# Carrying each half of the partitions on its own DMA queue, in 512-step chunks, in a matmul with a decayed running sum

## The chip, the cores and the metric

One core of a Trainium2 chip. The metric is the device time of one execution in microseconds (us), as the median of several runs. A shorter time is better.

## The reference

```python
B, S, D = (16, 2048, 1024)           # x: B x S x D, w: D x D, decay: D, all float32
xw = x @ w
out[:, 0, :] = xw[:, 0, :]
for t in range(1, S):
    out[:, t, :] = decay * out[:, t - 1, :] + xw[:, t, :]
```

x is 134 MB and so is the output; both have to pass between memory and SBUF once.

## The kernel before

The four quadrants of 32 partitions each hold a quarter of the channels. x comes in as float32 tiles `xf` of 512 time steps, ScalarE casts them to bfloat16 (`xb`), VectorE transposes them in 32x32 blocks (`xt`, the "input transpose"), TensorE multiplies with the weights into PSUM (`ps`), VectorE runs the decayed sum along time (the "scan", into `so`) and transposes back (`ot`, the "output transpose"), and `ot` is stored. A unit is 1024 steps of all 1024 channels: eight values of `n`, 16 matmuls each. All loads of x are issued on SyncE's queue, all stores on ScalarE's.

```python
def load(u, l):                                  # 512 steps: 2 MB
    xf = xfp.tile([128, 2, NI, CQ], FP32, name="xf")              # 3 buffers
    for r in range(2):
        for q in range(NQ):
            nc.sync.dma_start(out=xf[q * P:(q + 1) * P, r], in_=...)
    xb = xbp.tile([128, NI, CQ, 2], BF16, name="xb")              # 2 buffers
    for r in range(2):
        nc.scalar.copy(out=xb[:, :, :, r], in_=xf[:, r])
# ... turn(u, l): VectorE transposes xb into xt
for u, (b, h) in enumerate(units):
    for n in range(K):                           # K = 8
        ps = psp.tile([128, TU], FP32, name="ps")
        for k in range(K):
            for l in range(NL):
                nc.tensor.matmul(out=ps[:, l * TL:(l + 1) * TL], ...)
        # ... scan ps into so; keep its last column for the next unit
        if prev is not None:
            flush(prev)                          # output transpose of the scan before
            if n == 0:
                store(u - 1, prev[1])            # 4 dma_start on nc.scalar
        prev = (so, ot, n)
        if n == 1 and u + 1 < len(units):
            turn(u + 1, 0)
            load(u + 1, 1)
        if n == 5 and u + 1 < len(units):
            turn(u + 1, 1)
            if u + 2 < len(units):
                load(u + 2, 0)
```

The program's order is not the order on an engine: when the program is built, a scheduler places the instructions of each engine, VectorE's above all. In the profiles `ACTq` and `SPq` mark the issuing of transfers by ScalarE and SyncE, and `out_dram<-ot` is a store, `xf<-in_x_dram` a load of x.

## Time and profile before

| | before |
|---|---|
| median (lowest to highest) | 1121.59 us (1121.13 to 1122.7, 4 runs) |
| VectorE busy | 1013.7 us, 90% |
| TensorE busy | 932.3 us, 83% |
| ScalarE busy | 324.1 us, 29% |
| moved by DMA | 273.33 MB, mean 243 GB/s |
| 300 to 1060 us: VectorE busy, DMA | 752.47 of 760 us, 261 GB/s |

An engine's share of the whole span hides the stages: from 300 us on VectorE works without a pause, and its losses lie at the two ends. The lines behind this are in the prediction.

### The profile page before, as it was taken

The page shows a single profiled execution, that of the slowest core. Times are in us where ns is not written, and L with a number is a line of the kernel's source. Part 1 is how long each engine was busy: PE and PEld are TensorE (multiplying, and loading weights), DVE is VectorE, ACT ScalarE, POOL GpSimd, SP SyncE. Part 2 cuts the span into 40 slices and gives each one's busy share as a digit, 9 for nine tenths or more (in the row PEclk, how much of TensorE's full clock was granted, in tenths as well). Part 3 has the DMA queues.
Part 4 walks back from the last instruction along what each step waited for, and adds up shares of the span by engine and source line. Part 5 has one row for each costly group of instructions (what it writes and reads, how often), then busy time and mean ns, then how long its engine had stood idle before and what let it go on. Part 6 is the DMA issues. An engine that isn't in the chain of part 4 may idle for free.

```text
span 1123.0 us, 10242 instructions
## 1 busy us (share of the span) xinstructions
PE 932.3 (83%) x4096; PEld 408.4 (36%) x4096; DVE 1013.7 (90%) x584; ACT 324.1 (29%) x257; POOL 0.2 (0%) x4
## 2 busy tenths in 40 slices
PE   0287698796998998989898998989898998989880
PEld 0133243242443443434343443434343443434330
DVE  1295699798999999999999999999999999999991
ACT  2124122242422405151422405151422405151200
POOL 0000000000000000000000000000000000000000
PEclk9997799797999998999999899989999898999995
DMA  9949898999999999999999999999999999999777
GB/s 194 203 81 228 163 268 198 260 275 252 283 272 276 252 276 260 249 273 266 279 264 252 259 279 269 252 274 266 271 264 259 256 277 247 274 278 236 150 145 155
DMA packets 275056, 273.33 MB, mean 243 GB/s; under 512 B 11840, under 2 KB 273984, under 8 KB 275008
## 3 DMA queue, kind: packets, MB, share of 16 engines
q1 hardware_dynamic: 140800, 138.45, 55.5%
q10 hardware_dynamic: 134208, 134.23, 45.5%
q8 instruction: 32, 0.52, 0.2%
q14 instruction: 16, 0.13, 0.0%
HBM read 138.42 MB, written 134.22 MB: 243 GB/s over the span
## 4 chain that ended last, share of the span: by engine, by line
DVE 41%; DMA 27%; issue 9%; SPq 8%; PE 7%; ACTq 3%; ACT 2%; DVEq 0%
DVE so L141 24%; DMA xf<-in_x_dram 15%; DVE ot L115 11%; DMA out_dram<-ot 11%; SPq L91 8%; PE ps L133 7%; DVE xt L106 6%; ACTq L169 3%; ACT xb L97 2%; DMA xf<-in_w_dram 1%; DMA dec<-in_decay_dram 1%; SPq L76 0%; ACT keep L151 0%; ACTq L64 0%; DVE wsb L77 0%
## 5 line engine op out<-in xcount | busy, mean ns | idle before, releaser
L133 PE MATMUL ps<-xt,wsb 128*128 128x512 bf16 x4096 | 932.3, 389 | 157.7 <-DVE xt L106 95.0
L133 PEld LDWEIGHTS <-wsb 128*128 128x128 bf16 x4096 | 408.4, 100 | 681.0 <-issue 204.2
L97 ACT CAST xb<-xf 128x2048 bf16<-128x2048 f32 x128 | 310.8, 2474 | 306.2 <-DVE ot L115 100.3
L115 DVE STREAM_TRANSPOSE ot<-so 128x1024 f32<-128x1024 f32 x256 | 309.3, 1224 | 3.7
L141 DVE TENSOR_TENSOR_SCAN so<-dec,ps 128x1024 f32<-128x1024 f32 x128 | 285.3, 2252 | 20.6 <-PE ps L133 20.6
L141 DVE TENSOR_TENSOR_SCAN so<-dec,keep,ps 128x1024 f32<-128x1024 f32 x128 | 295.1, 2306 | 6.4 <-PE ps L133 6.4
L106 DVE STREAM_TRANSPOSE xt<-xb 128x2048 f32<-128x2048 f32 x64 | 146.2, 2285 | 44.6 <-ACT xb L97 42.7
L151 ACT COPY keep<-so 128x1 f32<-128x1 f32 x128 | 21.1, 186 | 429.7 <-DVE so L141 329.5
L77 DVE CAST wsb<-xf 128x1024 bf16<-128x1024 f32 x8 | 5.4, 687 | 9.8 <-DMA xf<-in_w_dram 9.8
L97 ACT ACT_TABLE_LOAD x1 | 1.3, 1283 | 8.8 <-DMA xf<-in_x_dram 8.8
L190 POOL MEMSET const-uint8-127<- 128x1 uint8 x1 | 0.1, 102 | 0.0
L190 POOL MEMSET const-bfloat16-1.0<- 128x1 bf16 x1 | 0.1, 101 | 0.0
L190 POOL MEMSET const-float32-0.0<- 128x1 f32 x1 | 0.1, 98 | 0.2 <-issue 0.2
L190 POOL MEMSET const-float32-1.0<- 128x1 f32 x1 | 0.1, 98 | 0.0
## 6 DMA issues: line engine op xcount, KB each, us to landing
xf<-in_x_dram SPq DMA_DIRECT2D x512, 256.0 KB, 8.3
out_dram<-ot ACTq DMA_DIRECT2D x128, 1024.0 KB, 13.3
xf<-in_w_dram SPq DMA_DIRECT2D x32, 128.0 KB, 4.0
dec<-in_decay_dram ACTq DMA_DIRECT2D x4, 1.0 KB, 5.6
```

Of the source, the lines that this page charges most:

```text
L77: nc.vector.tensor_copy(out=wsb[:, k].rearrange("p n q i -> p q n i"), in_=wv.rearrange("p (q n i) -> p q n i", q=NQ, n=K))
L91: nc.sync.dma_start(out=xf[q * P:(q + 1) * P, r], in_=_ap(x, [[2 * D, P], [64 * D, NI], [1, CQ]], (b * S + t0 + r) * D + q * CQ))
L97: nc.scalar.copy(out=xb[:, :, :, r], in_=xf[:, r])
L106: nc.vector.transpose(out=dst.rearrange("p k (i t) -> p i k t", t=P), in_=src.rearrange("p (i k t) -> p i k t", k=K, t=P))
L115: nc.vector.transpose(out=ot[:, :, n * P:(n + 1) * P], in_=so.rearrange("p (i t) -> p i t", t=P))
L133: nc.tensor.matmul(out=ps[:, l * TL:(l + 1) * TL], lhsT=wsb[:, k, n].rearrange("p q i -> p (q i)"), rhs=xt[:, k, l, :], start=(k == 0), st ...
L141: nc.vector.tensor_tensor_scan(out=so, data0=dec[:, n:n + 1].to_broadcast([128, TU]), data1=ps, initial=0.0 if h == 0 else last[n], op0=AL ...
L151: nc.scalar.copy(out=keep, in_=so[:, TU - 1:TU])
L169: nc.scalar.dma_start(out=_ap(out, [[D, P], [P * D, TU // P], [1, CQ]], (b * S + h * TU) * D + q * CQ), in_=ot[q * P:(q + 1) * P])
L190: nc = _bacc.Bacc("TRN2", target_bir_lowering=False, num_devices=1)
```

## The change

The intent: quadrants 0 and 1 (partitions 0 to 63) are always carried on SyncE's queue and 2 and 3 on ScalarE's, for loads and stores alike, so that the two queues never meet on the same half. The work goes in 512-step chunks; most groups are pairs of chunks (1024 steps, a unit as before), and the first two and last two chunks are groups of their own, so that the first scan starts sooner and the last store is smaller. The first chunk's matmuls run with k outermost, so that they can begin when the first slice of weights has come. Weights are cast on GpSimd, and so are the copies of the carried column.

```diff
+    def queue(q):
+        return nc.sync if q < 2 else nc.scalar
...
-    def load(u, l):
+    def load(c):
...
-            for q in range(NQ):
-                nc.sync.dma_start(
+            for q in (0, 2, 1, 3):
+                queue(q).dma_start(
...
+    groups = [[0], [1]] + [[c, c + 1] for c in range(2, nch - 2, 2)] + [[nch - 2], [nch - 1]]
...
+    def store(g, ot, n0, n1):
...
+        for q in (0, 2, 1, 3):
+            queue(q).dma_start(out=..., in_=ot[quad(q), :, n0 * P:n1 * P])
...
+    for gi, g in enumerate(groups):
...
+        at = {1: after[:1], 5: after[1:]}
...
+            scan(g, n, ps, ot)          # scan, then flush(): output transpose or store pending
+            for c in at.get(n, []):
+                turn(c)
+                if next_load < nch:
+                    load(next_load)     # four dma_start per queue, then two casts on ScalarE
+                    next_load += 1
...
+            pending.append(lambda g=g, ot=ot: store(g, ot, 0, K))
```

## The prediction

> **What bounds the kernel now.** I read the page first, then the busy times by stretch, then VectorE's timeline where the stretches differ, and the chain of waits last.
>
> From the page: busy time and share of each engine, then the costliest groups (busy us, mean ns, idle before, releaser).
>
> ```profile
> PE 932.3 (83%) x4096; PEld 408.4 (36%) x4096; DVE 1013.7 (90%) x584; ACT 324.1 (29%) x257; POOL 0.2 (0%) x4
> ...
> L115 DVE STREAM_TRANSPOSE ot<-so 128x1024 f32<-128x1024 f32 x256 | 309.3, 1224 | 3.7
> L141 DVE TENSOR_TENSOR_SCAN so<-dec,ps 128x1024 f32<-128x1024 f32 x128 | 285.3, 2252 | 20.6 <-PE ps L133 20.6
> ```
>
> VectorE (DVE) is the bound: 1013.7 of 1123.0 us. The by-stretch table says where the other 109 us lie (length, then busy PE, PEld, DVE, ACT, POOL, then granted clock, DMA share, GB/s):
>
> ```profile
> 0.00:46.00 46.00, 1.89 (x4) 0.58 (x5) 7.65 (x9) 10.88 (x5) 0.20 (x4) 1.00 1.00 198
> ...
> 173.00:236.00 63.00, 50.50 (x219) 21.65 (x217) 56.78 (x33) 21.16 (x14) 0.00 (x0) 0.86 0.97 251
> ...
> 428.00:491.00 63.00, 58.05 (x256) 25.50 (x255) 62.35 (x37) 19.48 (x16) 0.00 (x0) 0.96 1.08 266
> ...
> 1095.00:1123.00 28.00, 0.00 (x0) 0.00 (x0) 3.73 (x3) 0.00 (x0) 0.00 (x0) 0.50 0.75 155
> ```
>
> From about 300 to 1064 us VectorE is at 99% and a unit of 1024 steps takes 31.6 us (63.25 us a pair: the stores of two units begin at 376.55, 439.80, 503.24). 38 us are lost before 46 and 24 after 1095; the rest between 46 and 300, where this timeline shows the mechanism that I think decides the case (start, length, engine; idle and releaser in brackets):
>
> ```profile
> 199.99 2.31 DVE L141 TENSOR_TENSOR_SCAN so<-dec,keep,ps 128x1024 f32<-128x1024 f32 x1
> 202.33 1.25 DVE L115 STREAM_TRANSPOSE ot<-so 128x1024 f32<-128x1024 f32 x1
> 202.35 0.59 PE L133 MATMUL ps<-xt,wsb 128*128 128x512 bf16 x1 [2.92 <-DVE so L141]
> 203.50 2.27 DVE L106 STREAM_TRANSPOSE xt<-xb 128x2048 f32<-128x2048 f32 x1
> ...
> 205.82 10.46 PE L133 MATMUL ps<-xt,wsb 128*128 128x512 bf16 x37 [2.88 <-DVE xt L106]
> ...
> 211.57 2.29 DVE L141 TENSOR_TENSOR_SCAN so<-dec,ps 128x1024 f32<-128x1024 f32 x1 [5.80 <-PE ps L133]
> ```
>
> Here the second input transpose (xt) of a unit stands last on VectorE, just ahead of that unit's first scan. TensorE gets past its first matmul only when it is done, and VectorE waits 5.80 us for the 15 others. The same wait is 5.89 at 54.46, 6.40 at 98.31, 5.91 at 139.78. From 300 on it is gone: both xt transposes stand three or more scans before the unit's end (552.27: xt, then four scans in a row without a wait).
>
> **What the Trainium skill says.**
> 1. "TensorE: Matmul & The Clock Gate", Part 1 (the HAM clock gate): after an idle window of about 3.4 us the array runs at half rate until about 3.4 us of sustained work have passed. The trace agrees: the granted clock is 0.59 from 205.8 to 211.6 (17 matmuls) and 1.00 in the 5.4 us after (27). Hence 5.8 us for 15 matmuls, not 15 x 0.22 = 3.3.
> 2. "SBUF — State Buffer", Door 1: partitions 0 to 63 reach eight of the 16 DMA ports, 64 to 127 the other eight. That is the change's reason. The trace fits it: one queue alone moves about 206 GB/s (29 to 44 us), and with both at work stretches of 4 us show either 203 to 215 or 305 to 372, as if queues met on one half or not. The same page ("Can I just issue two DMAs to hit both halves?") says two loads at once gained only 6%; no run here shows that yet.
> 3. "GPSIMD Engine Reference", 3.1: elementwise work takes about twice VectorE's time. VectorE's weight cast is 0.69 us, so I estimate 1.4 us on GpSimd; the trace before has none there.
>
> **The change, part by part.** I also had the changed kernel built and read its instructions in order; the scheduler decides more than the diff.
>
> *VectorE's order* is the main term. Before, the late units run "xt, scan, scan, scan ..." in varied patterns with the transposes early. After, every one of the 30 pair groups has one fixed pattern: scan and output transpose three times, xt for the next group's first chunk, five more of both, xt for its second chunk, next group. The second xt is always immediately ahead of the next group's first scan. TensorE can do one matmul for each of n = 0 to 3 from the first chunk and then must wait, exactly as at 202 to 211 us. So each unit pays the 5.8 us, and TensorE, nearly idle before it, starts cold each time.
> A unit after: eight scans with output transposes, strictly alternating, 3.45 us apart without and 3.51 with a carried state (211.57 to 215.06 and on; 101.86 to 105.37), so 27.6 and 28.1, mean 27.8; two xt at 2.2 = 4.4; wait 5.8. Sum 38.0 us. Cross-check: the unit from 172.26 to 211.57 took 39.3 with one output transpose more (1.13), so 38.2. Against 31.6.
>
> *The start.* Lost: the 1024-step first unit that needs 4 MB of x and 4 MB of weights before it can run well (first scan at 54.46). After: 2 MB of x on two queues; ACT issues the upper weights only behind its casts of x (it runs in order), about 10 to 12 us; two slices fly at once at some 4 us (their landing time now), so eight need 16 us; last cast and k-step 3: first scan at about 31. Eight half-size scans and transposes, half of 3.45 plus 0.15 fixed (estimate): 15 us, to 46. xt of chunk 1 2.2, wait for eight cold matmuls at 0.43: 3.4; second group 15 + 2.2; then xt 2.2 and wait 5.8: first scan of the first pair at 77, where before it is at 98.31. Gain 21.
>
> *The end.* Half-size groups: xt and wait 5.6 once more. The last store is 1 MB on two queues, about 5 us, instead of 24 us for 4 MB on one. Gain 19.
>
> *Off the path.* keep copies go from ACT to GpSimd (128 x 0.19 us; the ACT waits of 329.5 us on the scans were harmless idle time). Casts of weights leave VectorE (5.4 us).
>
> *Sum.* 77, plus 29 units between the 30 first scans at 38.0 = 1102, gives 1179; last pair 27.8 + 2.2, to 1209; chunk 62 15, to 1224; 5.6, to 1230; chunk 63 15, to 1245; store 5: **1250 us**. As a difference: -21 at the start, -19 at the end, 6.4 x 29 = +186, less the 23 us that units lose today (971 us from the scan at 98.31 to that at 1069.64, where 30 x 31.6 is 948), and +7 for the split last unit: +130, the same to 3 us.
>
> **The rivals.**
> (a) *Transfers decide.* In the chain of waits DMA has 27%, and SyncE's queue waits 326.5 us for stores. If balanced ports and the shorter ends were all, VectorE's 1014 plus about 45 of start and 20 of end would make some 1080. Against: VectorE is at 99% in mid-run, where faster DMA gives it nothing, and the built order shows the late xt.
> (b) *ACT becomes the bound.* Its order after is: two stores, four loads, two casts, four loads, two casts. It waits in a cast for a load that it issued itself, so upper loads are never ahead by more than one chunk. Per unit: stores and loads on its ring 3.1 MB at about 206 GB/s 15 us, receipt 2, cast 2.5, then 1 MB 5, receipt 2, cast 2.5: about 30 us, under 38. If it took 42, the total would be some 1370. Against: casts would be ready some 15 us before the late xt.
> (c) *TensorE stays warm.* Then the wait is 3.3 to 3.6 instead of 5.8, 2.3 less x 30: about 1180. Against: it was cold in all four cases cited.
>
> **Range and chances.** The wait of 5.4 to 6.4 moves the sum by -12 to +18; the start by 8; alternation costs by 10; (b) in part adds, (c) in part takes away. 1200 to 1300 should hold it 8 times in 10. Faster by over 2% would need the late xt not to matter, though its order is fixed in the built program: 0.05. Within 2%: 0.04. Slower: 0.91.
>
> **What would show each step.** In the changed profile: VectorE's scan idle before, released by PE, some 170 us over about 30 waits near 5.8 us (now 27.0 in 5); granted clock near 0.6 in each of these gaps; VectorE near 82% busy in mid-run, a unit near 38 us; DMA about 225 GB/s there; first scan near 31 and first 1024-step scan near 77 us; under 10 us from the last transpose to the end. I am wrong if xt waits on ACT's cast instead (rival b), if waits are nearer 3.4 us (c), or if units stay near 32.

## The result, and the profile after

The changed kernel took 1405.03 us (1403.81 to 1405.84, 4 runs) against 1121.59 us: ratio 1.2524, 95% interval 1.2503 to 1.2546. Ratios are computed as the mean time of one kernel's fast runs over that of the other's of the same rounds, so they are not quite the ratio of the medians quoted. The direction was as predicted, but it is 155 us more than the 1250 us, and outside the range.

From the page after: busy time and share, then three groups (busy us, mean ns, idle before, releaser):

```profile
PE 985.0 (70%) x4015; PEld 417.2 (30%) x4096; DVE 1032.8 (74%) x608; ACT 315.8 (23%) x129; POOL 34.9 (2%) x156
...
L99 ACT CAST xb<-xf 128x2048 bf16<-128x2048 f32 x128 | 314.5, 2471 | 1034.9 <-DMA xf<-in_x_dram 905.4
...
L135 DVE TENSOR_TENSOR_SCAN so<-dec,ps 128x1024 f32<-128x1024 f32 (+1 forms) x128 | 279.7, 2186 | 101.2 <-PE ps L123 101.2
...
L105 DVE STREAM_TRANSPOSE xt<-xb 128x2048 f32<-128x2048 f32 x64 | 147.3, 2302 | 156.3 <-ACT xb L99 156.0
```

VectorE has the same work as before, to 20 us, but is busy for 74% of the span. The scans wait for TensorE, as predicted (101.2 us here and 96.1 in the group of carried scans, together 197.3 in 33 waits). What was not predicted is the last line: the input transposes wait 156.0 us for ScalarE's casts, and the casts wait 905.4 us for their loads (94.3 before).

VectorE's timeline of one unit, from the second input transpose of one group to the first scan of the next but one (start, length; in brackets idle and releaser):

```profile
621.21 2.31 DVE L105 STREAM_TRANSPOSE xt<-xb 128x2048 f32<-128x2048 f32 x1
628.86 2.29 DVE L135 TENSOR_TENSOR_SCAN so<-dec,ps 128x1024 f32<-128x1024 f32 x1 [5.33 <-PE ps L123]
...
645.43 2.31 DVE L105 STREAM_TRANSPOSE xt<-xb 128x2048 f32<-128x2048 f32 x1 [6.11 <-ACT xb L99]
...
673.11 2.35 DVE L135 TENSOR_TENSOR_SCAN so<-dec,keep,ps 128x1024 f32<-128x1024 f32 x1 [5.60 <-PE ps L123]
```

At 628.86 is the predicted wait for a cold TensorE. At 645.43 is the other: the *first* input transpose of the group, the one in mid-unit, stands still for 6.11 us until its cast is done. This unit, from 628.86 to 673.11, takes 44.25 us. On average over the run, from the first 1024-step scan at 79.63 to the last group's at 1328.74 us, it is 1249.1 / 29 = 43.1 us, where 38.0 were predicted and 31.6 were needed before.

The chain of waits of the changed kernel says what the cast waited for. It is read from the top down; each line is what released the next (start, length, what):

```profile
619.99 1.25 DVE ot L150
...
621.26 7.04 DMA out_dram<-ot
...
628.66 2.17 ACTq L93
...
630.87 11.98 DMA xf<-in_x_dram
...
642.92 2.49 ACT xb L99
...
645.43 0.04 DVE xt L105
...
663.76 1.26 DVE ot L150
...
665.03 7.03 DMA out_dram<-ot
```

This is a closed loop of 665.03 - 621.26 = 43.8 us: the group's store on SyncE's queue takes 7.0; ScalarE's queue, which was held until then, issues the next loads (2.5 with a small piece left out here); the load takes 12.0, the cast 2.5; then come the input transpose, five scans and their output transposes (VectorE, 18.3 from 645.43 to 663.76, and 1.3 for the last), and the last of these completes the group and allows the next store. A loop that closes on itself sets the pace whatever else the engines could do.

Why a load on ScalarE's queue waits for a store on SyncE's is in the packed trace, which names for each transfer the semaphore that its issue waits for and the one that its completion signals (`prof` doesn't print them). In the built program eight completion semaphores, numbers 99 to 106, serve the transfers of both queues and are used again and again. SyncE's store of 621.26 signals number 99 and lands at 628.30. The second of ScalarE's four loads is the next to use 99; it waits for it and is issued at 628.32, and the third and fourth stand behind it:

```profile
618.73 13.91 ACTq L93 DMA_DIRECT2D xf<-in_x_dram  x4
```

No buffer links this store and these loads. In the whole run 28 loads of ScalarE are issued within 60 ns of the landing of such a store of SyncE; in the kernels below that have the stores behind the loads it is at most 4.

In the two stretches from 300 to 1060 us, before and then after (length, busy PE, PEld, DVE, ACT, POOL with counts, then granted clock, DMA share, GB/s):

```profile
300.00:1060.00 760.00, 696.97 (x3092) 307.05 (x3091) 752.47 (x433) 236.34 (x191) 0.00 (x0) 0.96 1.06 261
```

```profile
300.00:1060.00 760.00, 529.78 (x2153) 223.37 (x2196) 564.81 (x317) 172.36 (x70) 12.65 (x69) 0.83 0.87 193
```

VectorE falls from 99% to 74%, and the transfers from 261 to 193 GB/s, although the change was meant to make them faster. The queues mostly took turns: by the packet records of the trace only SyncE's queue moves data from 622 to 634 us, and only ScalarE's from 644 to 648; in the 760 slices of 1 us each of the two moves over 20 GB/s in 223, one alone in 502. No engine is full: that is the mark of a loop of waits, not of a bound by one engine.

### The profile page after: what moved, and what is told of

It is laid out like the page before. It is cut to its first block, busy times and chain, and to the rows that moved or that the text cites. A ratio compares the mean times of both kernels' runs of the same rounds, so it can differ in the third digit from the quotient of the medians.

```text
span 1402.0 us, 10369 instructions
## 1 busy us (share of the span) xinstructions
PE 985.0 (70%) x4015; PEld 417.2 (30%) x4096; DVE 1032.8 (74%) x608; ACT 315.8 (23%) x129; POOL 34.9 (2%) x156
## 4 chain that ended last, share of the span: by engine, by line
DMA 40%; DVE 39%; issue 8%; ACT 5%; ACTq 4%; PE 2%; SPq 0%; DVEq 0%
DVE so L135 26%; DMA xf<-in_x_dram 25%; DMA out_dram<-ot 14%; DVE ot L150 10%; ACT xb L99 5%; ACTq L93 4%; DVE xt L105 3%; PE ps L123 2%; DMA wf<-in_w_dram 1%; DMA dec<-in_decay_dram 0%; SPq L93 0%; DVEq L233 0%; ACTq L99 0%; SPq L160 0%; DVEq L150 0%
## 5 line engine op out<-in xcount | busy, mean ns | idle before, releaser
L123 PE MATMUL ps<-xt,wsb 128*128 128x512 bf16 x4015 | 985.0, 403 | 405.6 <-DVE so L135 257.9
L123 PEld LDWEIGHTS <-wsb 128*128 128x128 bf16 x4096 | 417.2, 102 | 972.9 <-issue 530.1
L99 ACT CAST xb<-xf 128x2048 bf16<-128x2048 f32 x128 | 314.5, 2471 | 1034.9 <-DMA xf<-in_x_dram 905.4
L135 DVE TENSOR_TENSOR_SCAN so<-dec,keep,ps 128x1024 f32<-128x1024 f32 (+1 forms) x144 | 306.7, 2133 | 97.1 <-PE ps L123 96.1
L135 DVE TENSOR_TENSOR_SCAN so<-dec,ps 128x1024 f32<-128x1024 f32 (+1 forms) x128 | 279.7, 2186 | 101.2 <-PE ps L123 101.2
L150 DVE STREAM_TRANSPOSE ot<-so 128x1024 f32<-128x1024 f32 (+1 forms) x272 | 319.9, 1179 | 8.3
L105 DVE STREAM_TRANSPOSE xt<-xb 128x2048 f32<-128x2048 f32 x64 | 147.3, 2302 | 156.3 <-ACT xb L99 156.0
L145 POOL COPY keep<-so 128x1 f32<-128x1 f32 x144 | 26.4, 183 | 1314.0 <-DVE so L135 1314.0
L76 POOL CAST wsb<-wf 128x1024 bf16<-128x1024 f32 x8 | 8.3, 1037 | 22.7 <-DMA wf<-in_w_dram 22.5
```

Source lines behind the costliest of these rows:

```text
L76: nc.gpsimd.tensor_copy(out=wsb[:, k].rearrange("p n q i -> p q n i"), in_=wf.rearrange("p (q n i) -> p q n i", q=NQ, n=K))
L105: nc.vector.transpose(out=xt.bitcast(FP32).rearrange("p k (i t) -> p i k t", t=P), in_=src.rearrange("p (i k t) -> p i k t", k=K, t=P))
L123: nc.tensor.matmul(out=ps, lhsT=wsb[:, k, n].rearrange("p q i -> p (q i)"), rhs=xt[:, k, :], start=(k == 0), stop=(k == K - 1),)
L135: nc.vector.tensor_tensor_scan(out=so, data0=dec[:, n:n + 1].to_broadcast([128, T]), data1=ps, initial=0.0 if t0 == 0 else last[n], op0=AL ...
L145: nc.gpsimd.tensor_copy(out=keep, in_=so[:, T - 1:T])
L150: nc.vector.transpose(out=ot[:, :, n * P:(n + 1) * P], in_=so.rearrange("p (i t) -> p i t", t=P))
```

## The experiments

The question after the result is this: is there one cause (the late input transpose, only dearer than predicted) or are there two, each of which alone would hold the unit near 38 to 44 us? I call the second the **two-floors theory**: a unit takes the longer of (1) VectorE's order with its cold wait and (2) the loop of store, load, cast, transpose and scans. Fifteen kernels ran, in five batches. The results of all were correct.

All of them pin VectorE's order to the order of the program, as otherwise the scheduler could move instructions with each edit.

**Control: the pinning alone.** The edit reproduces the built order of the pair groups (in the cuts of code below, statements may stand on one line and comments are the document's):

```diff
+    with tc.manual_schedule(engines={mybir.EngineType.DVE}):
         for gi, g in enumerate(groups):
...
-        at = {1: after[:1], 5: after[1:]}
+            at = {2: after[:1], 7: after[1:]}
...
                 scan(g, n, ps, ot)
+                if len(g) == 2:
+                    flush()
```

> Control: the changed kernel with VectorE's order fixed as it was built (input transposes after the third and the eighth scan of a group), nothing else; all experiments were built on it, as otherwise the scheduler could move instructions. Both theories: 1405 us as the changed kernel, within 1% (1391 to 1419). If it differs by more, the experiments have to be compared with this one instead.

Measured: 1404.1 us (1401.81 to 1405.04), ratio to the kernel before 1.2524. Scans waited 184.7 us for TensorE and input transposes 170.7 for casts. It is the changed kernel, so the experiments can be compared with either.

### First batch: one of the two suspects at a time

**Matmuls of the first half first.** With the chunk l outermost, TensorE can do eight of the 16 matmuls of each n before the late input transpose.

```diff
-                    for k in range(K):
-                        for l in range(2):
+                    for l in range(2):
+                        for k in range(K):
                             matmul(ps[:, l * TL:(l + 1) * TL], n, k, xts[l])
```

> VectorE's order is pinned to that of the changed kernel; in each pair group TensorE now does all eight matmuls of the first chunk before those of the second, so only 8 instead of 15 stand between the late xt and the first scan. Prediction on record (the late xt and the cold TensorE set the pace): the wait before the first scan falls from 5.5 to about 3.4 us, the unit from 44.2 to about 42, the run to about 1340. Loop theory (VectorE's last output transpose, SyncE's store, the semaphore that ScalarE's next load waits for, the load, its cast, the middle xt, five more scans, and round again: about 43.7 us): the shorter wait is given back as a longer wait of the middle xt on the cast, the unit stays at 44 us, the run at 1390 to 1410.

Measured: 1432.78 us, above both expectations: 29 us more than the control, and 23 over the range of the loop theory. The wait for TensorE fell from 197.3 to 97.4 us in 30, and the time did not fall at all. These two lines of its waits (line, releaser, us in total, times, longest) show where it went:

```profile
DVE xt L105 <- ACT xb L99: 282.8, 57, 14.0
DVE so L135 <- PE ps L123: 97.4, 30, 15.4
```

The input transposes' wait rose from 156.0 to 282.8 us. What was taken from one floor was waited at the other, so the predicted cause is not what sets the time. Its chain is again a store (12.35 to 12.52 us, where the changed kernel's has 7.04), the load (9.4), the cast and five scans. The longer store fits the packed trace: here two of ScalarE's loads wait for semaphores of SyncE's stores, the later one, issued at 695.35, for that of the second store (landed 695.32).

**Fetching one chunk ahead.** `load` is split from `cast`; a chunk's load is issued one chunk before its casts, so ScalarE doesn't ask for a load and wait for it at once.

```diff
-    load(0); load_w(); load(1); turn(0)
+    load(0); cast(0); load_w(); load(1); load(2); cast(1); turn(0)
...
                     turn(c)
                     if next_load < nch:
                         load(next_load)
                         next_load += 1
+                    if c + 1 < nch:
+                        cast(c + 1)
```

> Both queues, VectorE's order and the late xt stay; only the issue of each chunk's loads moves one chunk ahead of its casts, so that ScalarE asks for chunk c+1 before it waits in the casts of chunk c. Loop theory: the middle xt no longer waits for its cast, what remains is VectorE's own work and the late xt, a unit of 38 us as in the prediction, the run 1210 to 1250. If the late xt alone set the pace, nothing changes: 1395 to 1410.

Measured: 1241.67 us; the input transposes waited 24.1 us in 3, the scans 174.2 in 31. With the loop opened this way the time is what the prediction gave for the late transpose alone.

**The queues undone.** All loads of x on SyncE's queue, all stores on ScalarE's, as before; the weights stay split.

```diff
-                queue(q).dma_start(          # loads of x
+                nc.sync.dma_start(
...
-            queue(q).dma_start(              # stores
+            nc.scalar.dma_start(
```

> Only the split of the transfers of x and out is undone: all loads of x on SyncE's queue, all stores on ScalarE's, as in the kernel before; chunks, ends, GpSimd's work and VectorE's pinned order (late xt) are those of the changed kernel. Loop theory: no load stands behind a store or a cast, so a unit of 38 us and a run of 1215 to 1260, the late xt being what is left. If the late xt alone set the pace: 1400.

Measured: 1255.02 us, 157.1 us of waiting for TensorE in 30, 34.8 for casts in 7. A load can no longer stand behind a store in its own queue, and the loop is gone; the late transpose stays.

**The mid-unit input transpose later.** After the sixth scan instead of the third.

```diff
-            at = {2: after[:1], 7: after[1:]}
+            at = {5: after[:1], 7: after[1:]}
```

> One thing only: VectorE does the middle xt after the sixth scan of a unit instead of after the third; queues, loads and the late xt stay. Loop theory: three scans and output transposes (10.5 us) leave the loop, which falls to about 33 us, under the 38 us of VectorE's own work with the late xt, so the run falls to 1220 to 1270. If ScalarE's own turn (store, load, cast, load, cast, each waiting for the one before) is what takes 44 us whatever VectorE does, the run stays near 1400. If the late xt set the pace, 1400 too.

Measured: 1340.07 us. This missed: the wait for casts fell only to 108.4 us. Its chain is a longer loop in place of the first: a store of 7.02 us, a load of 11.79, its cast, SyncE's load that was held until that cast had freed its buffer (10.94 and 3.67), the next cast, the late transpose, the scans. Giving one cast more time did not open the loop, it let another way round decide.

### Second batch: another opener, and both floors at once

**Casts on GpSimd.**

```diff
-            nc.scalar.copy(out=xb[:, :, :, r], in_=xf[:, r])
+            nc.gpsimd.tensor_copy(out=xb[:, :, :, r], in_=xf[:, r])
```

> ScalarE's casts of x move to GpSimd, so that ScalarE only issues transfers and never waits in a cast; queues, VectorE's order and the late xt stay. If what closes the loop is that ScalarE asks for the next load only after its casts, its loads now go out one to two chunks ahead and the loop opens: a unit of about 38 us, the run 1220 to 1270. If the loop needs only the shared queues (a load standing behind a store of the same queue), the run stays near 1400.

Measured: 1292.13 us; the cast takes 2.467 us there as on ScalarE; transposes waited 83.1 us for it. Freeing ScalarE's issuing from its casts opens the loop mostly, not wholly: 22 us over the expected range.

**Fetch-ahead and first half first together**, that is, both edits of the first batch:

```diff
+    load(0); cast(0); load_w(); load(1); load(2); cast(1); turn(0)
+                    for l in range(2):
+                        for k in range(K):
```

> The loads issued a chunk ahead (1241.7 us) and, on top, the order of the matmuls that left 8 instead of 15 behind the late xt; that order alone, with the loop closed, took 1432.8 against 1405. With the loop open the late xt is on the path: the wait falls by 2 to 3 us a unit, the run to 1150 to 1190. If it stays at 1240, the late xt is not what is left.

Measured: 1249.81 us. A clear miss: expected was that both floors would be gone. The wait for TensorE fell to 75.3 us, and that for casts rose again, from 24.1 to 125.8 in 28.

**Fetch-ahead and early input transposes together.** The transposes stand after the first and the fourth scan of a group, so TensorE has both chunks long before the next group.

```diff
-            at = {2: after[:1], 7: after[1:]}
+            at = {0: after[:1], 3: after[1:]}
```

> Loads a chunk ahead on the split queues, and VectorE does the two xt after the first and the fourth scan of a unit, so that four scans cover TensorE's start. With neither loop nor late xt a unit is VectorE's own 32.2 us: 1070 to 1090, faster than both kernels. If the queues, which take turns at 189 to 290 GB/s, can't bring 8.4 MB in 32 us, the run is 1100 to 1180.

Measured: 1255.08 us (1254.46 to 1255.27), ratio 1.1194 (1.1168 to 1.1221). A miss too, of both ranges. The late transpose is gone (16.4 us in one wait, the first), and 194.7 us of waiting for casts are there. Its chain (as above):

```profile
653.11 0.39 ACTq L165
...
654.29 17.02 DMA xf<-in_x_dram
...
672.54 2.46 ACT xb L104
...
691.16 0.39 ACTq L165
```

L165 is the store's issue. 1.2 us later the load is issued, and takes **17.02 us** where the median of ScalarE's loads, from issue to landing, is 7.6 to 8.9 in the kernels below that have the stores behind the loads: two 1 MB stores had been put into the same queue just ahead of it. The loop is 691.16 - 653.11 = 38.05 us. This fits the Trainium skill, "DMA: Bandwidth & Descriptors", section "Queues, rings and completion order": an issuing engine has one ring on each of the 16 DMA engines, and each is consumed in order.

But with fetch-ahead this load is for a later cast: the data of the casts at 670.20 and 672.54 had landed by 648.75. What stands before them in ScalarE's order is the issuing of the next loads. By the packed trace the third and fourth of these (668.77 and 669.84) wait for the completion semaphores of the second stores of SyncE and ScalarE (landed 668.75 and 669.82), and one at 671.33 for that of the long load (671.31). So the loop has a simpler root than ScalarE's casts: **stores are issued ahead of loads; some loads then stand behind them in their queue, others are not issued until a store has landed, and ScalarE's casts wait for the one or the other.**

**The queues undone and early input transposes:**

```diff
-                queue(q).dma_start(          # loads of x
+                nc.sync.dma_start(
-            queue(q).dma_start(              # stores
+            nc.scalar.dma_start(
+            at = {0: after[:1], 3: after[1:]}
```

> As the run with the queues undone (1255 us: loads on SyncE's queue, stores on ScalarE's), with the two xt after the first and fourth scan. The late xt costs 5.1 to 5.8 us a unit there, so 1075 to 1110. If it equals the run with split queues and early xt, the split brings nothing in mid-run; the start and the end differ by some 5 to 15 us.

Measured: 1111.65 us (1110.62 to 1111.66), ratio 0.9912 (0.9892 to 0.9932), 1.7 us over the expected range, and by the mark of 2% the same as the kernel before. Both floors are gone: between 280 and 1060 us VectorE is busy for 773.3 of 780. This left two readings: the split itself is harmful, or only the order of stores and loads.

### Third batch: the split, or the order within it

**Stores behind loads, split kept.** The fetch-ahead and early-transpose kernel, with the group's stores issued behind the load at the successor's fourth scan, ahead of its cast, instead of ahead of its first load.

```diff
-            pending.append(lambda g=g, ot=ot: store(g, ot, 0, K))
+            late.append(lambda g=g, ot=ot: store(g, ot, 0, K))
...
                     if next_load < nch:
                         load(next_load)
                         next_load += 1
+                    if n >= 3 or len(after) == 1:
+                        while late:
+                            late.pop(0)()
                     if c + 1 < nch:
                         cast(c + 1)
```

> The run with fetch-ahead and early input transposes on the two split queues (1255 us), with one thing more: a group's stores are now issued after the loads at its successor's fourth scan instead of ahead of its first loads, so each queue no longer carries 2 MB of stores in front of the load that the next cast waits for. Theory A (the load standing behind the stores in its own in-order queue makes the 38.05 us loop): the input transposes' wait on ScalarE's casts falls from 194.7 to under 60 us, a unit comes to the 8 x 3.47 + 2 x 2.2 = 32.2 us of VectorE's own work, the time to 1255 - 30 x 5.9 = about 1080 (1065 to 1120). Theory B (carrying loads and stores of each half together is itself the limit, whatever the order): 1220 to 1260.

Measured: 1084.05 us (1083.48 to 1085.86), ratio 0.9666 (0.9642 to 0.969). Moving the stores behind the loads took 171 us off the same kernel. The split is not harmful; the order was.

**The queues undone, with the ends mended.** x of the first four chunks and the stores of the last two groups on both queues; input transposes later in the two groups at the start.

```diff
-                nc.sync.dma_start(
+                (queue(q) if c < 4 else nc.sync).dma_start(
...
-            nc.scalar.dma_start(
+            (queue(q) if g[0] >= nch - 2 else nc.scalar).dma_start(
...
+            if gi < 2:
+                at = {4: after[:1], 7: after[1:]} if len(after) > 1 else {7: after}
```

> The run with all loads on SyncE's queue, all stores on ScalarE's and early input transposes (1111.65 us), with the two ends mended: the x of the first four chunks and the stores of the last two groups go over both queues by quadrant (as the change has it), and in the two single groups at the start the next input transpose stands later (after the last scan; for the first pair after the fifth and last). The waits of input transposes at 43.86, 63.46, 79.61 and 97.21 us, 25 us together, and 3.63 us at 1090.75 should shrink: first 1024-step scan near 73 instead of 88.90, some 15 us, and 4 to 5 at the end. Expected 1092 us (1085 to 1102), 0.974 of the kernel before. If nothing is gained, the mid-run has taken the losses back (a later limit on transfers), and the time stays near 1110.

Measured: 1098.44 us (1096.09 to 1099.99), ratio 0.9796 (0.9776 to 0.9817; at the mark of 2% this leaves open whether it is faster): in the expected range, but the first 1024-step scan was at 91.54 us, not near 73, since its transpose waited 12.09 us for a cast and the scan another 6.35 for TensorE. Of the two kernels of this batch the one with the split is faster by about 14 us. This is not a gain of the split in mid-run: VectorE is busy for 99% from 300 to 1060 us in both, and the mean unit is 32.3 us in both. 12.4 us lie before the first 1024-step scan (79.16 against 91.54) and 4.7 after the first scan of the last pair group, where both kernels use both queues, but differ in fetch-ahead, in the place of the input transposes and in the order of the stores.

### Fourth batch: the smallest repair

**An input transpose moved at the start.** In the first group it stands after the sixth scan.

```diff
-            at = {0: after[:1], 3: after[1:]}
+            at = {0 if gi else 5: after[:1], 3: after[1:]}
```

> The run with stores behind loads (1084 us), with one thing more: in the very first group the next input transpose stands after the sixth scan instead of after the first, where it waited 12.20 us for its cast at 46.49 us. Six half-size scans with transposes (1.78 us each) then fill 33 to 44 us, and some 2.7 of the 12.2 us of waiting stay: about 9 us less, 1075 us (1071 to 1080), 0.958 of the kernel before. If the first full group is held by TensorE or by transfers and not by this place, the time stays near 1084.

Measured: 1082.67 us (1081.08 to 1084.87), ratio 0.9647 (0.9626 to 0.9668). Nearly nothing gained: the intervals of this and of the kernel without the edit overlap. The 12.20 us of waiting at 46.49 us became four shorter ones, of 2.98, 2.98, 1.08 and 2.87 us, 9.9 together. In the profiled runs the first 1024-step scan came 5.8 us sooner (73.38 against 79.16), the end of the span 3.1. The start has another limit, which no run separates.

**No fetch-ahead.** Of all repairs only the early transposes and the stores' place are left.

```diff
     def load(c, stores=False):
         # ... issue the loads of chunk c
+        if stores:                       # true for the load at the fourth scan
+            while late:
+                late.pop(0)()
         # ... the two casts of chunk c, as in the changed kernel
```

> The run with stores behind loads (1084 us) without its fetch-ahead: again each load is issued together with its own casts, as in the changed kernel, so of the repairs only the early input transposes and the place of the stores (behind the load at the fourth scan) are left. If the stores' place is what made the loop long, then a load issued after the first scan has an otherwise empty queue, lands some 7 us later, is cast in 2.5 us, and is just in time for the transpose three scans (10.5 us) on: 1085 to 1130 us. If fetching ahead is what counts: every load-to-cast chain is exposed, 1200 us or more.

Measured: 1083.3 us (1081.44 to 1083.44), ratio 0.9646 (0.9629 to 0.9663): as fast as with fetch-ahead, and 1.7 us under the expected range. Fetching ahead, which took 163 us off the changed kernel in the first batch, is worth nothing once the stores stand behind the loads. From its page and its by-stretch table (columns as above):

```profile
PE 932.7 (86%) x4096; PEld 408.4 (38%) x4096; DVE 1023.5 (95%) x608; ACT 314.7 (29%) x129; POOL 34.9 (3%) x156
```

```profile
280.00:1060.00 780.00, 702.68 (x3099) 308.42 (x3099) 773.42 (x444) 225.15 (x92) 19.06 (x104) 0.97 1.00 256
```

VectorE is the bound again, at 95% of a span of 1081.3 us and 99% in mid-run. A unit, from one first input transpose to the next (631.47 and 663.52 in its timeline), is about 32.1 us: the work of eight scans, eight output and two input transposes with no wait.

### Fifth batch: the missing cells of the square

Two edits, the transposes' place and the stores' place, were known to be enough together. The last batch tried each alone.

**Late transposes, stores behind loads** (at the successor's third scan, as there the load stands):

```diff
             at = {2: after[:1], 7: after[1:]}
-            pending.append(lambda g=g, ot=ot: store(g, ot, 0, K))
+            late.append(lambda g=g, ot=ot: store(g, ot, 0, K))
+                        load(next_load, n >= 2)     # stores between its issue and its casts
```

> The changed kernel with one thing changed: a group's stores are issued behind the loads at its successor's third scan instead of ahead of them; the late second input transpose stays. Two-floors theory: the store-load-cast loop opens and the late transpose with its 5.8 us of cold TensorE is left: unit 38 us, scans wait for TensorE about 170 us in 30, input transposes for casts under 50, time 1240 us (1225 to 1265), which is what the prediction said of the whole change. If the loop does not come from the stores' place (but from casts and loads sharing ScalarE): 1330 us or more.

Measured: 1239.95 us (1238.36 to 1240.92), ratio 1.1061 (1.1043 to 1.108). The scans waited 168.9 us for TensorE in 30, the input transposes 21.2 in 3. VectorE's timeline:

```profile
608.00 2.35 DVE L139 TENSOR_TENSOR_SCAN so<-dec,keep,ps 128x1024 f32<-128x1024 f32 x1 [5.33 <-PE ps L127]
...
618.57 2.27 DVE L108 STREAM_TRANSPOSE xt<-xb 128x2048 f32<-128x2048 f32 x1
...
645.66 2.29 DVE L139 TENSOR_TENSOR_SCAN so<-dec,ps 128x1024 f32<-128x1024 f32 x1 [5.08 <-PE ps L127]
```

The unit is 37.7 us and the mid-unit transpose at 618.57 waits for nothing. These are the unit and the time that the prediction had worked out.

**Early transposes, stores ahead of loads:**

```diff
-            at = {2: after[:1], 7: after[1:]}
+            at = {0: after[:1], 3: after[1:]}
```

> The changed kernel with the other thing changed alone: input transposes after the first and the fourth scan, stores still ahead of the loads. Two-floors theory: the wait for TensorE goes, but the load behind 2 MB of stores in its own queue takes 17 us (as measured with fetch-ahead), then 2.5 for the cast, 2.2 for the transpose, and without fetch-ahead that transpose is the one after the fourth scan, so five scans of 3.5 us follow until the next store: about 41 us a unit, 1340 us (1290 to 1400), the wait of input transposes for casts over 200 us. If the late transpose is the whole cause: 1080 to 1100, since with the stores moved as well it was 1083.

Measured: 1385.75 us (1385.24 to 1385.99), ratio 1.2363 (1.2344 to 1.2381). Its chain:

```profile
622.36 2.31 DVE xt L105
...
639.10 15.16 DMA out_dram<-ot
654.27 0.02 issue
654.29 5.39 DMA xf<-in_x_dram
...
662.06 2.46 ACT xb L99
...
664.55 0.04 DVE xt L105
```

Here the stores take 15.16 us, and the load comes after them (ScalarE's third load, issued at 654.29, waits for the semaphore of SyncE's second store): 664.55 - 622.36 = 42.2 us a unit. No scan but the first waits for TensorE; the input transposes wait 325.8 us for casts in 32.

| | stores ahead of loads | stores behind loads |
|---|---|---|
| late input transposes | 1404.1 us, unit 43.1 | 1239.95 us, unit 37.7 |
| early input transposes | 1385.75 us, unit 42.3 | 1083.3 us, unit 32.4 |

The units are means of the 29 from the first pair group to the last.

Removing the late transpose alone gives 18 us, moving the stores alone 164, both together 321. If the causes added up, both would give 182. Two floors do not add: the unit takes the larger one, and the lower one shows only when the upper is gone.

## Why the prediction was right or wrong

- **Start: right, in part by luck.** First scan 32.99 us (31 predicted), first 1024-step scan 79.63 (77). Between the two, errors offset each other: the first group took 13.7 us for 15, and the wait of the second group, at 55.13, was 6.19 for 3.4.
- **End: right.** From the end of the last output transpose, at 1395.69, to the end of the span at 1402.0 are 6.3 us (5 predicted, 24 before). From the last group's first scan to the end of the span are 73.3 us, where the sum has 71.
- **The wait for cold TensorE: right.** 197.3 us in 33 waits (some 170 in 30 predicted); at 628.86 and 673.11 it is 5.33 and 5.60. In the three stretches of 4 us from 616 to 628 the granted clock is 0.50, 0.50 and 0.58, then 1.00, so rival (c) is out. Its dismissal claimed more than the trace before shows: the clock is 0.53 to 0.59 in three of the "four cases cited", but reads 1.00 before 54.46, though its 16 matmuls took as long.
- **The unit of 38.0 us: wrong for this kernel.** It is 43.07. All of the error lies here: 29 x (43.07 - 38.0) = 147 of the 152 us between 1250 and the profiled span of 1402.0. With the stores moved the same unit is 37.7 and the total 1239.95, so the arithmetic of the late transpose was good, and what failed was to take it as the only floor.
- **The step that failed is in rival (b):** "Per unit: stores and loads on its ring 3.1 MB at about 206 GB/s 15 us, receipt 2, cast 2.5, then 1 MB 5, receipt 2, cast 2.5: about 30 us, under 38", and its dismissal, "casts would be ready some 15 us before the late xt". The sum counts only the transfers and casts. It does not ask what starts the store: VectorE's last output transpose of the group, which in turn waits for the scans behind the mid-unit input transpose, which waits for the cast. The measured loop of 43.8 us has 24.0 us of store, issue, load and cast (7.04, 2.49, 11.98 and 2.49) and some 19.6 us of VectorE's own work, which was left out. It also sums each queue alone: in the loop ScalarE's loads wait for a store on SyncE's queue. And the cast that came late was that of the *first* chunk, at 645.43, not of the second; the dismissal looked at the wrong transpose. For a unit of 42 us the text gave "some 1370": the run with a unit of 42.2 took 1385.75.
- **A reading of the transfers: wrong.** The text takes stretches of 203 to 215 GB/s as having "both at work". By the packet records of the trace before, in each of these stretches (240 to 248, 256 to 260, 272 to 280, 288 to 292 and 304 to 312 us) one queue moved all or nearly all of the data.
- **Rival (a), some 1080, was not this kernel but it was reachable:** 1083.3 us with two things moved.
- **VectorE near 82% in mid-run and 225 GB/s:** 74% and 193 in the changed kernel. In the run with only the stores moved it is 644.52 of 760 us, 85%, at 225 GB/s.

What stays open: the square shows that the place of the stores closes the loop. That it does so through the shared completion semaphores is read from the traces; no run gave the queues semaphores of their own, so how much of the time is theirs, and how much comes from standing behind stores in one queue, is not shown. Nor is it shown which part of the two repairs' remaining start could still go: without fetch-ahead, VectorE is idle for some 45 us before 280 us.

## What to carry to other kernels

When a change puts loads and stores into the same queues, look at the order in which they are issued, and at which completion semaphores the built program uses twice: here a store issued ahead of loads put its time into them, in its own queue and, by a shared semaphore, in the other. To predict the pace of a steady loop, close the loop: follow each wait back until you come to the same instruction one round earlier, through every engine, and sum the whole way round; a per-engine or per-queue sum is only a lower bound. And if two floors lie close together, test the two edits in a square: one alone can look nearly worthless (18 us here), the other gains 164, and both together are worth 321.

## What the Trainium skill lacked or had wrong

- "SBUF — State Buffer", section "Can I just issue two DMAs to hit both halves?", gives +6% for two transfers on the two halves. Here, in the run with fetch-ahead and early transposes, the stretches of 656 to 660 and 660 to 664 us, with both queues at work on their own halves, show 350 and 347 GB/s; from 672 to 684, where the packet records show mostly one queue at work, it is 201 to 207. That is 1.7 times. (The first are stores, the second loads. From 644 to 648 us of the changed kernel, one queue alone with a store shows 190. Loads of x and weights alone, at the start of the changed kernel, show 206 to 260 GB/s.)
- "DMA: Bandwidth & Descriptors", section "Rules for kernel authors", says that two transfers to disjoint partition halves are not worth it, and that spreading transfers over the issuing engines only saves issue time. The 350 GB/s above speak against the first for bandwidth; whether it gains time is not shown. The kernel with the split (1084.05 us) beat the one with a queue for loads and one for stores (1098.44) by 14 us, but their mean unit is the same (32.3 us), and at the ends, where the gain lies, they differ in more than the queues.
- "GPSIMD Engine Reference", 3.1, measures GpSimd at about twice VectorE's time, for an addition of two inputs; it has no figure for a cast. The weight cast, with one input, took 1.037 us on GpSimd and 0.687 on VectorE, 1.5 times; the prediction, which carried the factor over, had estimated 1.4 us.
- No page that I read tells what a load costs that was issued behind stores in its own queue: 17.02 us here for one behind 2 MB of stores, against a median of 8.4 in the kernel with the stores behind and no fetch-ahead.
